# Query, key and value transposes in the tile's own projection banks, in a two-layer trunk kernel

## The chip, the core and the metric

One core of a Trainium2 chip runs the whole program. The metric is the device time of one execution in microseconds (us), given as the median of several executions. The engines are TensorE (PE in the profile; PEld are its weight loads), VectorE (DVE), ScalarE (ACT), GpSimd (POOL) and SyncE (SP), which issues most of the transfers. Matrix results land in PSUM; the kernel takes it in eight pieces of 128 partitions by 512 float32 numbers, called banks here, two of which it uses together as one tile of 1024.

## The reference

One inference step of a trunk of two layers, on 640 tokens (512 "sample" tokens and 128 "prompt" tokens that share the weights), with model width 2048 and heads of 128. Each layer normalises and modulates its input, takes one wide input projection, mixes, gates, and takes one output projection:

```
hp = rms_norm(xp, norm_g[layer]) * (1.0 + sc_p) + sh_p
hs = rms_norm(xs, norm_g[layer]) * (1.0 + sc_s) + sh_s
qa, ka, va, ga, ub, bb, cb, gb = split_cols(h @ w_in, EVEN_SPLIT)
q = rms_norm(q_heads(qa, A_KV, A_GROUP), qn)
k = rms_norm(kv_heads(ka, A_KV), kn)
o = banded_attend(apply_rope(q, cos, sin), apply_rope(k, cos, sin), v, ctx[0], ctx[1], sink_g)
```

The even layer has banded attention (8 query heads on 2 key heads) and a gated short convolution; the odd layer has a differential attention (8 queries and 8 keys, 4 values of double width) and a dense attention (8 queries on 2 keys). Sample tokens also read 256 cached keys and values per head. Queries and keys are divided by the root of the mean of their squares (QK-norm) and, for sample tokens, rotated. Keys and values of the prompt are outputs too.

## The kernel before

**Tiles.** A job is one tile of 128 projection columns for all 640 tokens. The tile lies with its columns on the partitions, in two halves of 320 tokens, `pa` and `pb`, each in a bank of its own. `new_pp` (L283) hands out the banks: tags `pa0`, `pb0`, `pa1`, `pb1`, one buffer each, or, for one index, the two banks of the score tile S. A tile is the sum over 16 blocks of 128 input features; inputs and weights are split into a high and a low part in float32r, so each block is three matmuls per half (L263 to L265, in parts L277 to L279, 96 matmuls to a tile). `split` writes the high part on ScalarE (L227) and the low part on VectorE (L228); it splits weights (`wh`, `wl`) and everything else alike. Another part of the input projection of the odd layer, and of both output projections, forms two tiles together from sums of blocks (L596 to L598). TensorE does little besides these matmuls.

**PSUM.** Four banks are `pa` and `pb`; two are S, which a block's scores fill (L812 to L814), and out of which the exponentials are taken (`p`, L786); two are places with the tag T (`psT`, L64). All else goes through the two T places: transposes of keys and values to rows (`to_rows`, L621, matmul at L625), sums of squares of a query (L708), their transposes (L716), transposes of `p` (L800, split to `pth` and `ptl`), a block's output (L860 to L862), and a few sums for the modulation.

**The generators.** When a tile's matmuls are done, its job runs as a generator that is advanced by one step at each slot between quarters of the next tiles:
- `k_gen` (L639) copies the key from its banks to SBUF (`stg`, in `stage`), starts the load of the cached keys (`ctxk`), transposes the five token blocks to rows (L625; four of the sample into one place, the prompt's into another), takes squares on ScalarE and multiplies by the norm's gain on VectorE (`kg`, L657), scales by the root (L664), rotates (`m`, L674), and some slots later transposes back. In that last part the two blocks of the cache (L682), the four of `m` and the last of `kg` (both L625) each take a T place, one after another, and each is split into the key's operands (`k0h`, `k0l`).
- `q_gen` (L692) writes the query and its squares to SBUF (`qx`, `qsq`), rotates it, sums the squares over the partitions by three matmuls with ones (L708, a T place), copies the sums (`qs`, L711), transposes them (L716, another T place), and splits the query.
- `v_gen` and `v_kept` transpose a value to rows through `v_rows` (L737) and split it. `v_gen` is for values that come straight from their banks, `v_kept` for values that were kept in DRAM.
- `pair_gen` takes the ten blocks of scores of two queries.
- Two of the odd layer's keys come back as kept tiles from DRAM (`places` in `k_gen`), with no bank; the others are staged from their banks as in the even layer.

In the first tiles of the even layer six columns are summed up in SBUF (`sums`, TRANS), while two, the first key and another, stay in banks. A fill (`fill0`: L203, L205) works off the modulation weights of later parts on VectorE, in slots of its own rate; its loads (`adaw`, L200) are on SyncE's queue with the weights' (`raw`).

**Order.** The program is written in the order of slots. A scheduler of the framework then sets each engine's order from program order, dependencies and its own model of when a buffer comes free; a tile that waits for a T place may so be moved behind matmuls of the next projection, and another place changes where it stands.

Of the kernel before, what the change touches and what calls it, by code (L numbers as in the profile page):

```python
# [11 lines left out]
F32 = mybir.dt.float32  # L12
# [8 lines left out]
P = 128  # L21
D = 2048
KT = D // P
NS = 512
NP = 128
NT = NS + NP
HALF = NT // 2
CTX = 256
# [22 lines left out]
def trunk_kernel(ctx: ExitStack, tc: tile.TileContext, I: dict, O: dict):  # L51
    nc = tc.nc
    V, A, PE, G = nc.vector, nc.scalar, nc.tensor, nc.gpsimd
# [6 lines left out]
    pproj = ctx.enter_context(tc.tile_pool(name="pproj", bufs=1, space=PSUM))  # L60
# [3 lines left out]
    def psT():  # L64
        return pT.tile([P, 512], F32, tag="T", name="T")
# [21 lines left out]
    ident = const.tile([P, P], F32, name="ident")  # L87
# [138 lines left out]
    def split(hi, lo, x):  # L226
        A.activation(hi, x, AF.Copy)  # L227
        V.tensor_sub(lo, x, hi)  # L228
# [54 lines left out]
    def new_pp(i):  # L283

        if i == 2:
            t = pS.tile([P, 1024], F32, tag="S", name="Sp")
            return t[:, 0:512], t[:, 512:1024]
        return tuple(pproj.tile([P, 512], F32, tag=f"p{h}{i}", name=f"p{h}") for h in "ab")


    prep, attn, early = [], [], []
# [8 lines left out]
    def release(tag):  # L300
        while any(tag in getattr(g, "tags", ()) for g in attn):
            advance(attn, 1)
# [312 lines left out]
    def stage(ap, pp):  # L615
        s = ap.tile([P, NT], F32, tag="stg", name="stg", bufs=2)
        for i, sl in HV:
            A.copy(s[:, sl], pp[i][:, 0:HALF])
        return s

    def to_rows(src, sample):  # L621

        t = psT()
        for i, b in enumerate(range(4) if sample else (4,)):
            PE.transpose(t[:, i * P:(i + 1) * P], src(b), ident)  # L625
        return t if sample else t[:, 0:P]

    def cols_of(t):
        return lambda b: t[:, b * P:(b + 1) * P]
# [9 lines left out]
    def k_gen(ap, pp, tag, src, gain, new_out, then=None, more=0, places=None):  # L639
        def place(c, b, name):  # L640
            if places is None:
                return ap.tile([P, b, P], F32, tag="rp", name=name, bufs=3)
            return places[:, c:c + b, :]

        raw = ap.tile([P, 2, P], F32, tag="ctxk", name="ctxk", bufs=1)
        nc.sync.dma_start(raw, src.rearrange("(c p) d -> p c d", p=P))
        x = stage(ap, pp) if places is None else pp
        yield
        ss = small.tile([P, 5], F32, tag="ss", name="ss")
        kg = place(0, 5, "kg")  # L650
        junk = ap.tile([P, P], F32, tag="junk", name="junk", bufs=1)
        for sample in (True, False):
            t = to_rows(cols_of(x), sample)
            for i, b in enumerate(range(4) if sample else (4,)):
                A.activation(junk, t[:, i * P:(i + 1) * P], AF.Square, accum_out=ss[:, b:b + 1])
            if sample:
                V.tensor_mul(kg[:, 0:4, :], t.rearrange("p (b f) -> p b f", b=4),  # L657
                             gain[:, None, :].to_broadcast([P, 4, P]))
            else:
                V.tensor_mul(kg[:, 4, :], t, gain)  # L660
        r = small.tile([P, 5], F32, tag="r", name="r")
        V.tensor_scalar(ss, ss, 1.0 / P, EPS, ALU.mult, ALU.add)
        G.tensor_tensor(r, ss, half[:, 0:5], op=ALU.pow)
        V.tensor_mul(kg, kg, r[:, :, None].to_broadcast([P, 5, P]))  # L664
        nc.gpsimd.dma_start(new_out, kg[:, 4, :])
        m1, m2 = place(5, 4, "m1"), place(9, 4, "m2")
        x = kg[:, 0:4, :].rearrange("p b (a h f) -> p (b a) h f", a=2, h=2)
        y = m1.rearrange("p b (a h f) -> p (b a) h f", a=2, h=2)
        z = m2.rearrange("p b (a h f) -> p (b a) h f", a=2, h=2)
        V.tensor_mul(y, x, cosR[:, :, None, :].to_broadcast([P, 8, 2, 32]))  # L670
        V.scalar_tensor_tensor(out=z[:, :, 0, :], in0=x[:, :, 1, :], scalar=-1.0, in1=sinR,
                               op0=ALU.mult, op1=ALU.mult)
        V.tensor_mul(z[:, :, 1, :], x[:, :, 0, :], sinR)
        V.tensor_add(m1, m1, m2)  # L674
        for _ in range(2 + more):
            yield
        release(tag)
        hi, lo = (ap.tile([P, 896], F32R, tag=tag + t, name=tag + t) for t in "hl")
        st[tag] = (hi, lo)
        t = psT()  # L680
        for c in range(2):
            PE.transpose(t[:, c * P:(c + 1) * P], raw[:, c, :], ident)  # L682
        split(hi[:, 0:CTX], lo[:, 0:CTX], t[:, 0:CTX])
        t = to_rows(lambda b: m1[:, b, :], True)
        split(hi[:, CTX:CTX + NS], lo[:, CTX:CTX + NS], t)
        t = to_rows(lambda b: kg[:, b, :], False)
        split(hi[:, CTX + NS:CTX + NT], lo[:, CTX + NS:CTX + NT], t)
        if then:
            prep.append(then())


    def q_gen(ap, pp, tag, gain, then=None, wait=True):  # L692
        x = ap.tile([P, NT], F32, tag="stg", name="qx", bufs=2)
        sq = ap.tile([P, NT], F32, tag="stg", name="qsq", bufs=2)
        for i, sl in HV:
            A.activation(x[:, sl], pp[i][:, 0:HALF], AF.Copy, scale=gain)
            A.activation(sq[:, sl], pp[i][:, 0:HALF], AF.Square)
        sw = ap.tile([P, NS], F32, tag="rp", name="qsw", bufs=3)
        for d in range(4):
            A.copy(sw[32 * d:32 * d + 32, :], x[32 * (d ^ 1):32 * (d ^ 1) + 32, 0:NS])  # L700
        V.tensor_mul(sw, sw, sinT)
        m = ap.tile([P, NS], F32, tag="rp", name="qm", bufs=3)
        V.tensor_mul(m, x[:, 0:NS], cosT)
        V.tensor_add(m, m, sw)
        yield
        ss = psT()
        for g, o in enumerate((0, 256, 384)):
            PE.matmul(ss[32 * g:32 * g + 32, 0:256], ones, sq[:, o:o + 256], start=True, stop=True,  # L708
                      tile_position=(0, 32 * g))
        sb = ap.tile([96, 256], F32, tag="qs", name="qs", bufs=1)  # L710
        A.copy(sb, ss[0:96, 0:256])  # L711
        if wait:
            yield
        t = psT()
        for j in range(2):
            PE.transpose(t[:, j * 96:(j + 1) * 96], sb[:, j * P:(j + 1) * P], ident[0:96, 0:96])  # L716

        u = small.tile([P, 6], F32, tag="ss", name="u")
        V.tensor_scalar(u.rearrange("p (j g) -> p j g", j=2),
                        t[:, 0:192].rearrange("p (j g x) -> p j g x", j=2, g=3)[:, :, :, 0], P * EPS, None, ALU.add)  # L720
        release(tag)
        r6 = small.tile([P, 6], F32, tag="r" + tag, name="r" + tag, bufs=1)
        G.tensor_tensor(r6, u, half[:, 0:6], op=ALU.pow)
        r = [r6[:, c:c + 1] for c in (0, 3, 1, 4, 5)]
        hi, lo = (ap.tile([P, NT], F32R, tag=tag + t, name=tag + t) for t in "hl")
        split(hi[:, 0:NS], lo[:, 0:NS], m)
        split(hi[:, SPLIT], lo[:, SPLIT], x[:, SPLIT])
        st[tag] = (hi, lo, r)
        if then:
            attn.append(then())  # L730

    def ctx_load(ap, src, w):
        raw = ap.tile([P, 2, w], F32, tag="ctxv", name="ctxv", bufs=1)
        nc.sync.dma_start(raw, src.rearrange("(c p) d -> p c d", p=P))
        return raw

    def v_rows(ap, x, hi, lo, cols, new_out):  # L737
        t = to_rows(cols_of(x), True)
        split(hi[:, 2:6, cols], lo[:, 2:6, cols], t.rearrange("p (b f) -> p b f", b=4))
        t = to_rows(cols_of(x), False)  # L740
        vp = ap.tile([P, P], F32, tag="vp", name="vp", bufs=1)
        V.tensor_copy(vp, t)
        split(hi[:, 6, cols], lo[:, 6, cols], vp)
        nc.gpsimd.dma_start(new_out, vp)

    def v_tiles(ap, w):
        release("v")
        st["v"] = tuple(ap.tile([P, 7, w], F32R, tag=t, name=t) for t in ("vh", "vl"))
        return st["v"]

    def v_gen(ap, pp, src, new_out):
        x = stage(ap, pp)
        yield
        hi, lo = v_tiles(ap, P)
        split(hi[:, 0:2, :], lo[:, 0:2, :], ctx_load(ap, src, P))
        v_rows(ap, x, hi, lo, slice(0, P), new_out)

    def v_load(i):
        t = pools["cur"].tile([P, NT], F32, tag="vraw", name="vraw", bufs=1)
# [268 lines left out]
    def k_job(tag, src, gain, new_out, *a):  # L1028
        return lambda pp: k_gen(pools["cur"], pp, tag, src, gains[gain], new_out, *a)
# [96 lines left out]
    for i in range(4):  # L1126
        kv, h = i // 2, 2 * i
# [554 lines left out]
    for n in range(1, 4):  # L1682
        h = heads[n]
# [118 lines left out]
```

## Time and profile before

| | |
|---|---|
| median of 3 runs | 2285.19 us (2284.16 to 2288.55) |
| profiled execution | 2283.79 us, its span 2282.0 us |
| TensorE busy | 2249.8 us, 15941 instructions |
| VectorE busy | 1603.5 us, 2830 instructions |
| ScalarE busy | 1087.7 us, 2281 instructions |
| HBM | 150 GB/s over the span |

The span is the part of the profiled execution between its first and its last instruction on the core; the execution's own time is 1.8 us longer. Times in rows are us from the start of the span. A row of the timeline gives a start, the busy time, the engine, the line, the operation with what it writes and reads, how many were joined into the row, and in brackets how long the engine waited ahead of it and for which instruction of which engine. A row of the waits gives the waiting instruction, an arrow, the instruction that ended the wait, and total, count and longest.

### The profile page before, as it was taken

Reading aid. Unit: us, or ns where it says so; the run is one execution under the profiler, and the core shown is the slowest. Engines: PE = TensorE matmul, PEld = TensorE weight load, DVE = VectorE, ACT = ScalarE, POOL = GpSimd, SP = SyncE. Lnnn points to the kernel's source line nnn. Section 1 sums busy time; section 2 is a strip of 40 time slices with the busy share of each in tenths; the row PEclk is TensorE's granted clock in tenths of the full one; section 3 lists DMA queues with packets and bytes.
Section 4 is the critical chain, followed back from the end, with each engine's and each line's share of the span. In section 5 each row is a group of like instructions: output and inputs, shape, how many; then the busy total and the mean of one; then the engine's idle time right before and its main releaser. Section 6 shows DMA issues by size and latency. Waiting matters only on the chain.

```text
span 2282.0 us, 41084 instructions
## 1 busy us (share of the span) xinstructions
PE 2249.8 (99%) x15941; PEld 2172.7 (95%) x15941; DVE 1603.5 (70%) x2830; ACT 1087.7 (48%) x2281; POOL 162.1 (7%) x226
## 2 busy tenths in 40 slices
PE   7999999999999999999999999999999999999999
PEld 5889999999999999999999999999999999999999
DVE  5666969779779777887797666566666655557765
ACT  5224545244352222544474444465565676755443
POOL 1001000000000000000100001111111100000101
PEclk9999999999999999999999999999999999999999
DMA  9975555555537564855553334423223211238642
GB/s 322 318 227 181 171 155 170 184 155 172 179 112 242 176 190 142 273 171 148 165 166 102 116 116 115 141 65 100 85 62 99 71 55 58 74 102 272 183 136 62
DMA packets 385395, 344.20 MB, mean 151 GB/s; under 512 B 16418, under 2 KB 342528, under 8 KB 384688
## 3 DMA queue, kind: packets, MB, share of 16 engines
q1 hardware_dynamic: 370624, 296.66, 43.5%
q0 software_dynamic: 13856, 42.76, 5.4%
q8 instruction: 125, 2.05, 0.4%
q10 hardware_dynamic: 720, 2.16, 0.3%
q14 instruction: 70, 0.57, 0.1%
HBM read 301.93 MB, written 39.59 MB: 150 GB/s over the span
## 4 chain that ended last, share of the span: by engine, by line
PE 48%; ACT 3%; DVE 2%; DMA 2%; issue 2%; POOL 0%; SPq 0%; POOLq 0%; DVEq 0%; ACTq 0%
PE pq L598 7%; PE pq L597 7%; PE pq L596 7%; PE pb L278 2%; PE pb L277 2%; PE pb L279 2%; PE pa L277 2%; PE pa L279 2%; PE pa L278 2%; PE T L800 1%; PE S L812 1%; PE T L625 1%; PE S L814 1%; PE S L813 1%; ACT qsw L700 1%
## 5 line engine op out<-in xcount | busy, mean ns | idle before, releaser
L227 ACT ACTIVATE wh<-raw 128x512 fp32r<-128x512 f32 x418 | 263.6, 631 | 550.7 <-PE pb L264 393.6
L228 DVE TENSOR_TENSOR wl<-raw,wh 128x512 fp32r<-128x512 f32 x418 | 287.5, 688 | 201.5 <-ACT wh L227 177.7
L263 PE MATMUL pa<-h,wh 128*128 128x320 f32 x978 | 309.9, 318 | 1.8 <-ACT h L227 1.7
L264 PE MATMUL pa<-h,wh 128*128 128x320 f32 x978 | 304.0, 312 | 1.4 <-DVE h L228 1.3
L265 PE MATMUL pa<-h,wl 128*128 128x320 f32 x978 | 303.0, 310 | 0.0
L264 PE MATMUL pb<-h,wh 128*128 128x320 f32 x978 | 302.6, 309 | 0.0
L265 PE MATMUL pb<-h,wl 128*128 128x320 f32 x978 | 302.4, 309 | 0.0
L263 PE MATMUL pb<-h,wh 128*128 128x320 f32 x978 | 301.6, 309 | 0.7 <-ACT h L1412 0.7
L205 DVE SCALAR_TENSOR_TENSOR acc<-adaw,sT,acc 128x1024 f32<-128x1024 f32 x240 | 300.1, 1276 | 0.5 <-DMA adaw<-in_ada_w 0.5
L596 PE MATMUL pq<-h,wh 128*128 128x320 f32 x672 | 208.8, 311 | 0.5 <-ACT wh L227 0.5
L598 PE MATMUL pq<-h,wl 128*128 128x320 f32 x672 | 207.9, 309 | 0.2 <-DVE wl L228 0.2
L597 PE MATMUL pq<-h,wh 128*128 128x320 f32 x672 | 207.7, 309 | 0.0
L263 PEld LDWEIGHTS pa<-h,wh 128*128 128x128 f32 x978 | 183.6, 188 | 15.1 <-issue 9.1
L264 PEld LDWEIGHTS pa<-h,wh 128*128 128x128 f32 x978 | 183.8, 188 | 7.2 <-issue 4.1
L263 PEld LDWEIGHTS pb<-h,wh 128*128 128x128 f32 x978 | 183.3, 188 | 1.4 <-ACT h L1412 0.9
L264 PEld LDWEIGHTS pb<-h,wh 128*128 128x128 f32 x978 | 183.6, 188 | 0.9 <-issue 0.8
L265 PEld LDWEIGHTS pa<-h,wl 128*128 128x128 f32 x978 | 183.7, 188 | 0.4 <-issue 0.4
L265 PEld LDWEIGHTS pb<-h,wl 128*128 128x128 f32 x978 | 183.6, 188 | 0.0
L598 PE MATMUL pq<-T,wl 128*128 128x320 f32 x504 | 155.1, 308 | 0.2 <-DVE wl L228 0.2
L596 PE MATMUL pq<-T,wh 128*128 128x320 f32 x504 | 155.2, 308 | 0.1
L597 PE MATMUL pq<-T,wh 128*128 128x320 f32 x504 | 155.2, 308 | 0.0
L277 PE MATMUL pa<-h,wh 128*128 128x320 f32 x448 | 146.1, 326 | 0.0
(463 smaller groups left out, 5408.1 us busy)
## 6 DMA issues: line engine op xcount, KB each, us to landing
adaw<-in_ada_w SPq DMA_DIRECT2D x128, 512.0 KB, 4.2
raw<-in_ev_w_in SPq DMA_DIRECT2D x176, 256.0 KB, 3.3
raw<-in_od_w_in SPq DMA_DIRECT2D x154, 256.0 KB, 2.9
ada<-in_ada_w SPq DMA_DIRECT2D x32, 1024.0 KB, 9.7
w<-in_od_w_in SPq DMA_DIRECT2D x27, 512.0 KB, 3.9
yd<-y POOLq DMA_DIRECT2D x32, 320.0 KB, 3.5
yin<-yd SPq DMA_DIRECT2D x32, 320.0 KB, 4.5
w<-yd SPq DMA_DIRECT2D x32, 320.0 KB, 4.2
```

The source lines that it names most:

```text
L205: V.scalar_tensor_tensor(out=acc[c], in0=w, scalar=sT[:, kt, c:c + 1], in1=acc[c], op0=ALU.mult, op1=ALU.add)
L227: A.activation(hi, x, AF.Copy)
L228: V.tensor_sub(lo, x, hi)
L263: PE.matmul(ps, wh[:, i, :], hi[:, sl], start=(j == js[0] if alone else (pos == 0 and j == 0)), stop=False)
L264: PE.matmul(ps, wh[:, i, :], lo[:, sl], start=False, stop=False)
L265: last_mm[j % 4] = PE.matmul(ps, wl[:, i, :], hi[:, sl], start=False, stop=(j == js[1] - 1 if alone else (pos == 3 and j == 3)))
L277: PE.matmul(ps, wh[:, j, :], hi[:, sl], start=(qd == 0 and j == 0), stop=False)
L278: PE.matmul(ps, wh[:, j, :], lo[:, sl], start=False, stop=False)
L279: PE.matmul(ps, wl[:, j, :], hi[:, sl], start=False, stop=(qd == 3 and j == 3))
L596: PE.matmul(ps, wh[:, j, :], hi, start=(new and h == 0 and j == 0), stop=False, **kw)
L597: PE.matmul(ps, wh[:, j, :], lo, start=False, stop=False, **kw)
L598: PE.matmul(ps, wl[:, j, :], hi, start=False, stop=(h == 1 and j == 3), **kw)
```

## The change

Four edits. A list `whole` holds the projection tiles that have banks of their own (not those in S or in SBUF), and `bank_of(pp, i)` gives bank `i` of such a tile, or a T place for any other. With it
- `k_gen` transposes a key's sample rows into the key's own `pa` and its prompt rows into its own `pb`;
- `q_gen` puts the sums of squares into the query's own `pa` and their transposes into its own `pb`;
- `v_gen` transposes a value's rows into its own `pa` and `pb`;
- in the last part of `k_gen` the last block of `kg` goes into the T place of the two cache blocks (L690, L691), so that two places are used where there were three, and it is split ahead of `m`.

Lines from 286 on stand 8 lower in the kernel after (L708 is L716 there, L625 is L633). The number of instructions of every engine stays the same but for waits.

```diff
@@ -285,7 +285,15 @@
         if i == 2:
             t = pS.tile([P, 1024], F32, tag="S", name="Sp")
             return t[:, 0:512], t[:, 512:1024]
-        return tuple(pproj.tile([P, 512], F32, tag=f"p{h}{i}", name=f"p{h}") for h in "ab")
+        pp = tuple(pproj.tile([P, 512], F32, tag=f"p{h}{i}", name=f"p{h}") for h in "ab")
+        whole.extend(pp)
+        return pp
+
+    whole = []
+
+    def bank_of(pp, i):
+
+        return pp[i] if any(t is pp[i] for t in whole) else psT()
 
 
     prep, attn, early = [], [], []
@@ -618,9 +626,9 @@
             A.copy(s[:, sl], pp[i][:, 0:HALF])
         return s
 
-    def to_rows(src, sample):
-
-        t = psT()
+    def to_rows(src, sample, t=None):
+
+        t = psT() if t is None else t
         for i, b in enumerate(range(4) if sample else (4,)):
             PE.transpose(t[:, i * P:(i + 1) * P], src(b), ident)
         return t if sample else t[:, 0:P]
@@ -650,7 +658,7 @@
         kg = place(0, 5, "kg")
         junk = ap.tile([P, P], F32, tag="junk", name="junk", bufs=1)
         for sample in (True, False):
-            t = to_rows(cols_of(x), sample)
+            t = to_rows(cols_of(x), sample, bank_of(pp, 0 if sample else 1))
             for i, b in enumerate(range(4) if sample else (4,)):
                 A.activation(junk, t[:, i * P:(i + 1) * P], AF.Square, accum_out=ss[:, b:b + 1])
             if sample:
@@ -680,11 +688,11 @@
         t = psT()
         for c in range(2):
             PE.transpose(t[:, c * P:(c + 1) * P], raw[:, c, :], ident)
+        PE.transpose(t[:, CTX:CTX + P], kg[:, 4, :], ident)
         split(hi[:, 0:CTX], lo[:, 0:CTX], t[:, 0:CTX])
+        split(hi[:, CTX + NS:CTX + NT], lo[:, CTX + NS:CTX + NT], t[:, CTX:CTX + P])
         t = to_rows(lambda b: m1[:, b, :], True)
         split(hi[:, CTX:CTX + NS], lo[:, CTX:CTX + NS], t)
-        t = to_rows(lambda b: kg[:, b, :], False)
-        split(hi[:, CTX + NS:CTX + NT], lo[:, CTX + NS:CTX + NT], t)
         if then:
             prep.append(then())
 
@@ -703,7 +711,7 @@
         V.tensor_mul(m, x[:, 0:NS], cosT)
         V.tensor_add(m, m, sw)
         yield
-        ss = psT()
+        ss = bank_of(pp, 0)
         for g, o in enumerate((0, 256, 384)):
             PE.matmul(ss[32 * g:32 * g + 32, 0:256], ones, sq[:, o:o + 256], start=True, stop=True,
                       tile_position=(0, 32 * g))
@@ -711,7 +719,7 @@
         A.copy(sb, ss[0:96, 0:256])
         if wait:
             yield
-        t = psT()
+        t = bank_of(pp, 1)
         for j in range(2):
             PE.transpose(t[:, j * 96:(j + 1) * 96], sb[:, j * P:(j + 1) * P], ident[0:96, 0:96])
 
@@ -734,10 +742,10 @@
         nc.sync.dma_start(raw, src.rearrange("(c p) d -> p c d", p=P))
         return raw
 
-    def v_rows(ap, x, hi, lo, cols, new_out):
-        t = to_rows(cols_of(x), True)
+    def v_rows(ap, x, hi, lo, cols, new_out, banks=(None, None)):
+        t = to_rows(cols_of(x), True, banks[0])
         split(hi[:, 2:6, cols], lo[:, 2:6, cols], t.rearrange("p (b f) -> p b f", b=4))
-        t = to_rows(cols_of(x), False)
+        t = to_rows(cols_of(x), False, banks[1])
         vp = ap.tile([P, P], F32, tag="vp", name="vp", bufs=1)
         V.tensor_copy(vp, t)
         split(hi[:, 6, cols], lo[:, 6, cols], vp)
@@ -753,7 +761,7 @@
         yield
         hi, lo = v_tiles(ap, P)
         split(hi[:, 0:2, :], lo[:, 0:2, :], ctx_load(ap, src, P))
-        v_rows(ap, x, hi, lo, slice(0, P), new_out)
+        v_rows(ap, x, hi, lo, slice(0, P), new_out, [bank_of(pp, i) for i in range(2)])
 
     def v_load(i):
         t = pools["cur"].tile([P, NT], F32, tag="vraw", name="vraw", bufs=1)
```

The scheduler sets another order with it. Below is what stands in a row on an engine at three places; `[waits ...]` names what the instruction waits for, and "x3" joins equal ones.

TensorE at the first key of the even layer, before. `stg` is the staged key, `ctxk` its cached keys, `kg` the key in rows; `pb<-h_...` is the end of one projection tile, and `pa<-h_469` the first block of the next in the key's banks.

```order
L625 MATMUL T<-ident,stg 128x128 [waits PE_49]
...
L263 MATMUL pb<-h_2059,wh 128x320
L264 MATMUL pb<-h_2059,wh 128x320
L265 MATMUL pb<-h_2059,wl 128x320
L263 MATMUL pa<-h_469,wh 128x320
L264 MATMUL pa<-h_469,wh 128x320
L265 MATMUL pa<-h_469,wl 128x320 [waits DVE_49]
```

The same place after.

```order
L633 MATMUL pa<-ident,stg 128x128 [waits Activation_49]
L633 MATMUL pa<-ident,stg 128x128
L633 MATMUL pb<-ident,stg 128x128
...
L265 MATMUL pb<-h_2059,wl 128x320
L690 MATMUL T<-ident,ctxk 128x128 [waits DMAHW5_49,PE_49]
L690 MATMUL T<-ident,ctxk 128x128
L263 MATMUL pa<-h_469,wh 128x320 [waits DVE_49]
...
L263 MATMUL pa<-h_764,wh 128x320
L691 MATMUL T<-ident,kg 128x128 [waits DVE_49]
```

The key's transposes lie in `pa` and `pb` and wait for no matmul of before; the opening matmul of the next tile now waits for VectorE, the cache's transposes stand 16 projection matmuls earlier, ahead of it, and the transpose of `kg` stands ten matmuls behind the opener, 39 matmuls earlier than before.

TensorE in the odd layer at a query, before. `qsq` are the query's squares; `pth`, `pb<-h_13104` and the like belong to the attention block and to the projection that run beside it (numbers of buffers differ between the two kernels: 13104 there is 13084 here).

```order
L279 MATMUL pa<-h_13120,wl 128x320
L277 MATMUL pa<-h_13128,wh 128x320
L278 MATMUL pa<-h_13128,wh 128x320
L279 MATMUL pa<-h_13128,wl 128x320
L708 MATMUL T<-qsq,ones 32x256 [waits DVE_49]
L708 MATMUL T<-qsq,ones 32x256 x2
L277 MATMUL pb<-h_13104,wh 128x320
L278 MATMUL pb<-h_13104,wh 128x320
L279 MATMUL pb<-h_13104,wl 128x320
L860 MATMUL T<-pth,vh 128x256 [waits Activation_49]
```

The same place after.

```order
L808 MATMUL T<-ident,p 128x128 x3
L277 MATMUL pb<-h_12827,wh 128x320
L278 MATMUL pb<-h_12827,wh 128x320
L279 MATMUL pb<-h_12827,wl 128x320
L716 MATMUL pa<-qsq,ones 32x256 x3
L277 MATMUL pa<-h_13084,wh 128x320
...
L277 MATMUL pb<-h_13084,wh 128x320
L278 MATMUL pb<-h_13084,wh 128x320
L279 MATMUL pb<-h_13084,wl 128x320
L868 MATMUL T<-pth,vh 128x256 [waits Activation_49]
```

The sums stand ahead of the twelve `pa` matmuls instead of behind them, and wait for nothing new; the next block's L860 (L868) stands where it stood.

VectorE in the even layer from the first instruction of the fill, before. `nm` is a score's maximum, `l` and `rl` its sum and reciprocal, `acc` the fill's accumulators.

```order
L203 TENSOR_SCALAR acc_2931<-adaw,sT 128x1024 [waits DMAHW0_49,DMASW3_49,DMASW2_49]
L790 TENSOR_TENSOR l<-l,es 128x1 [waits Activation_49]
L203 TENSOR_SCALAR acc_2932<-adaw,sT 128x1024
L792 RECIPROCAL rl<-l 128x1 [waits DVE_49]
L205 SCALAR_TENSOR_TENSOR acc_2931<-adaw,sT,acc_2931 128x1024 [waits DMAHW1_49]
L779 TENSOR_REDUCE nm<-S 128x1 [waits PE_49]
L228 TENSOR_TENSOR wl<-raw,wh 128x512 [waits DMAHW5_49,Activation_49]
L783 TENSOR_SCALAR nm<-nm,rq_2705,nsink 128x1 [waits DVE_49,Pool_49]
```

The same place after.

```order
L203 TENSOR_SCALAR acc_2928<-adaw,sT 128x1024 [waits DMAHW0_49,DMASW3_49,DMASW2_49]
L203 TENSOR_SCALAR acc_2929<-adaw,sT 128x1024
L798 TENSOR_TENSOR l<-l,es 128x1 [waits Activation_49]
L205 SCALAR_TENSOR_TENSOR acc_2928<-adaw,sT,acc_2928 128x1024 [waits DMAHW1_49,DVE_49]
L800 RECIPROCAL rl<-l 128x1 [waits DVE_49]
L205 SCALAR_TENSOR_TENSOR acc_2929<-adaw,sT,acc_2929 128x1024
L787 TENSOR_REDUCE nm<-S 128x1 [waits PE_49]
L228 TENSOR_TENSOR wl<-raw,wh 128x512 [waits DMAHW5_49,Activation_49]
L791 TENSOR_SCALAR nm<-nm,rq_2702,nsink 128x1 [waits DVE_49,Pool_49]
```

Each step of the fill stands one place earlier, so that ahead of the second `nm` stand two L205 where there was one.

## The prediction

> **What bounds the kernel now.** I read the page first, then TensorE's waits by line, then the timelines around each wait.
>
> ```profile
> PE 2249.8 (99%) x15941; PEld 2172.7 (95%) x15941; DVE 1603.5 (70%) x2830; ACT 1087.7 (48%) x2281; POOL 162.1 (7%) x226
> PEclk9999999999999999999999999999999999999999
> 1200.00:1300.00 100.00, 100.00 (x684) 100.00 (x683) 68.03 (x103) 46.07 (x88) 4.32 (x8) 1.00 0.36 111
> ```
>
> The last row is one stretch: its length, then busy us and instructions of TensorE, its weight loads, VectorE, ScalarE and GpSimd, the clock, DMA share and GB/s. TensorE is busy nearly all of the 2282.0 us at a full clock. In an undisturbed stretch 684 matmuls start in 100 us: 0.146 us a step, which prices an early or late place in its order. The change adds no work (engine by engine the order has as many instructions as before), so it can only move TensorE's waits. They are these:
>
> ```profile
> PE T L708 <- DVE ptl L228: 1.5, 3, 0.6
> PE S L812 <- ACT p L786: 1.1, 4, 0.5
> PE T L625 <- DVE k0l L228: 1.0, 1, 1.0
> PE T L708 <- DVE kpl L657: 0.8, 2, 0.4
> PE T L800 <- ACT p L871: 0.7, 1, 0.7
> PE T L625 <- DVE m L674: 0.6, 1, 0.6
> ```
>
> Columns: total us, times, longest. L708 writes a query's sums, L625 a transpose; where they wait for `ptl`, `k0l` or `kpl`, they need none of these, but the T place (one of two) that the named instruction still reads. That is 1.5 + 0.8 + 1.0 = 3.3 us. The `m` wait is for data.
>
> **The change: q sums.** For 22 of the 24 queries the sums go to bank pa of the query's own projection (the other two have theirs in SBUF, so no bank). In the order shown above for the query near 1896 us the wait on VectorE is gone, and the sums stand 11 or 12 matmuls earlier at three such places (L708 is L716 now).
>
> ```profile
> 1895.66 0.69 DVE L228 TENSOR_TENSOR ptl<-T,pth 128x512 fp32r<-128x512 f32 x1
> 1896.41 0.63 PE L708 MATMUL T<-qsq,ones 128*32 128x256 f32 x6 [0.52 <-DVE ptl L228]
> 1897.39 0.35 ACT L711 COPY qs<-T 96x256 f32<-96x256 f32 x1
> 1897.52 0.28 PE L860 MATMUL T<-pth,vh 128*128 128x256 f32 x1
> ```
>
> `ptl` ends at 1896.35 and frees the place. What is late next is L860 to L862, which read this `pth` and `ptl`; 0.52 us earlier they would start at 1897.00, still behind `ptl`. So the wait goes and does not come back: 2.3 us in the five places (1.5 + 0.8).
>
> **Key's third place.** The last key transpose (`kg`) joins the cache's two in one place.
>
> ```profile
> 462.82 0.60 PE L625 MATMUL T<-ident,m 128*128 128x128 f32 x4
> 464.73 0.31 PE L264 MATMUL pa<-h,wh 128*128 128x320 f32 x1
> 465.58 1.01 DVE L228 TENSOR_TENSOR k0l<-T,k0h 128x256 fp32r<-128x256 f32 x2
> 466.05 0.33 PE L625 MATMUL T<-ident,kg 128*128 128x128 f32 x1 [1.01 <-DVE k0l L228]
> 466.51 0.31 PE L264 MATMUL pb<-h,wh 128*128 128x320 f32 x1
> 1555.94 0.31 PE L277 MATMUL pa<-h,wh 128*128 128x320 f32 x1
> 1556.21 0.33 PE L625 MATMUL T<-ident,kg 128*128 128x128 f32 x1
> 1556.66 0.31 PE L277 MATMUL pa<-h,wh 128*128 128x320 f32 x1
> 1566.93 0.66 PE L625 MATMUL T<-ident,m 128*128 128x128 f32 x4
> ```
>
> In a row of four a transpose takes (0.60 - 0.27)/3 = 0.11 us, 0.27 being one alone as recorded. Alone between projection matmuls, `kg` cost 464.73 to 466.51 less three steps of 0.146, so 1.34 us, and 0.28 us at 1556. In the row it costs 0.11. That gives 1.34 - 0.11 = 1.2 us once, and 0.17 us at the six other single places, 1.0 us. At three more places it now stands inside TensorE's wait for `m` (as before 1566.93), so that its 0.11 us goes, 0.3 us in all.
>
> **Remainder.** The second transpose of a query's sums goes to pb and value transposes to pa and pb. The rows of the waits name nothing of size there; I take 0.5 us, with bounds of 0 and 1.0 (the latter twice the wait at 1896). Gains: 2.3 + 1.2 + 1.0 + 0.3 + 0.5 = 5.3 us, with bounds of 4.8 and 5.8.
>
> **What it costs: the first key.** Here the change adds a wait. The order at it is shown above. The opening matmul takes the bank in which the key now lies, only 8 projection matmuls after its transposes, so it waits until VectorE has read the key; and `kg` stands ten matmuls on, waiting for its scaling. Behind these two waits stands the whole projection.
>
> ```profile
> 200.38 0.31 PE L263 MATMUL pa<-h,wh 128*128 128x320 f32 x1
> 201.73 0.69 DVE L657 TENSOR_TENSOR kg<-T,gain_rows 128x512 f32<-128x512 f32 x1
> 204.10 0.82 DVE L664 TENSOR_TENSOR kg<-kg,r 128x640 f32<-128x640 f32 x1 [1.13 <-POOL r L663]
> 208.58 0.66 PE L625 MATMUL T<-ident,m 128*128 128x128 f32 x4 [0.64 <-DVE m L674]
> ```
>
> The opener came at 200.38; with two transposes ahead (0.22) it comes at 200.60 and waits until 202.42: 1.8 us. Ten steps later, at 203.9, it waits for the scaling's end at 204.92: 1.0 us. The old wait for `m` (0.64) goes, since VectorE reaches `m` two weight splits sooner; `kg` and one value transpose standing alone add 0.17. So TensorE is 1.8 + 1.0 - 0.6 + 0.2 = 2.4 us late here. A part is then absorbed, because two later waits hang on VectorE:
>
> ```profile
> 224.68 0.89 DVE L635 SCALAR_TENSOR_TENSOR y<-gt_t,sum 128x320 f32<-128x320 f32 x2
> 225.63 0.82 SPq L200 DMA_DIRECT2D adaw<-in_ada_w  x2
> 229.90 0.75 DVE L203 TENSOR_SCALAR acc<-adaw,sT 128x1024 f32<-128x1024 f32 x1 [2.08 <-DMA adaw<-in_ada_w]
> 231.38 1.26 DVE L205 SCALAR_TENSOR_TENSOR acc<-adaw,sT,acc 128x1024 f32<-128x1024 f32 x1
> 235.03 0.39 PE L812 MATMUL S<-k0h,q0h 128*128 128x256 f32 x1 [0.54 <-ACT p L786]
> 237.49 0.88 PE L800 MATMUL T<-ident,p 128*128 128x128 f32 x6 [0.67 <-ACT p L871]
> 240.00:300.00 60.00, 60.00 (x434) 59.08 (x434) 57.68 (x99) 25.47 (x56) 1.66 (x3) 1.00 0.60 181
> ```
>
> The fill (L203, L205, the modulation weights) starts when its first load lands, 4.27 us after L635 lets it go. L635 follows the second query's sums, but ScalarE's order there is looser now; I take 0.8 us late, between 0 and 2.4. And VectorE's order moved, as shown above: one L205 more (1.26) stands ahead of the second score's maximum. So this chain runs 0.8 + 1.26 = 2.0 us late, about as late as TensorE, and the two waits shrink little. But the six transposes of 237.49 now stand four matmuls (0.6 us) later, so work fills that wait: TensorE leaves it 2.0 - 0.6 = 1.4 us late. Bounds: 0.7 (load not late at all) and 3.0 (load late by the full 2.4). I take 1.4.
>
> **Sum.** -5.3 + 1.4 = -3.9 us. The profiled execution took 2283.79 (2282.0 of span and 1.8 around it), 1.4 below the median of 2285.19; applied to the median, 2281.3 us. 0.2% is 4.6 us, about the spread of the three runs (4.4 us) and what a measurement of this kernel can tell from no change.
>
> **The rule of the Trainium skill that speaks against this.** At all other tiles the order leaves 60 to 72 matmuls, 8.8 to 10.5 us, between the last sums or transposes in a bank and the projection that takes it next, and at 1897.39 the reader came one us after the sums. The Trainium skill (Perfetto Trace Analysis, Optimizing Tensor Performance) says that independent groups of matmuls should rotate through different PSUM banks, so that emptying one overlaps the next. By that rule the projections would wait. The trace bears it out for the first key alone.
>
> **Rivals.**
> - *The early wait is absorbed whole.* If VectorE's slack after 230 us takes it up, as it would if the load were not late and the fill fell behind, -5.3 us: 2279.9. For it: two waits lie there. Against it: VectorE is busy 57.68 of 60 us behind. Chance 0.15.
> - *The sums' waits come back.* If the transposes of the next block wait in their stead, 2.3 us is not gained: -1.6 us, 2283.6. For it: ScalarE and VectorE feed the same blocks. Against it: L860's inputs above. Chance 0.22.
> - *Slower: VectorE's queue becomes the bound from 230 to 300 us.* If each of the eight scores after the first two waits behind one more L205, 8 x 1.26 = 10.1 us on top of -3.9: 2291.4. It decides where TensorE's slack per score is under 1.26 us. For it: 57.68 of 60. Against it: the one-off shift of the fill, and no wait of size named there. Chance 0.10.
> - *Slower: the rotation rule everywhere.* 33 tiles have such work in their banks (22 queries, 10 keys, a value). If each of the 32 beside the first key's cost 1.8 us as there, that is 58 us, 2339. For it, only that key's place; against it, 8.8 us of distance and a reader that comes after one. Chance 0.01.
>
> **How the numbers follow.** The forecast has the remaining 0.52, with 2279.5 to 2283.0 as its own range. Faster by over 0.2% means under 2280.6: the first rival and somewhat under half of the forecast, 0.38. Slower: the last two, 0.11. Same: 0.51. The range runs from 2277.5, below the first rival by the runs' spread of about 2 us, to 2287.5, halfway between the second rival and the third; the slower rivals stay out.
>
> **What would show it.** Right: no wait of L716 (L708 before) or `kg` on a T place; near 200 us one of L263 on `kg` of 1.8 us and one of L691 of 1.0; the waits of L820 and L808 near 238 us not longer. Wrong: new waits of L808 or L820 between 238 and 300 us, or of an opening matmul elsewhere on ACT or DVE.

## The result and the profile after

The changed kernel takes 2282.97 us (median of 22 runs, 2280.11 to 2289.43), the kernel before 2285.61 us (22 runs beside them, 2282.78 to 2291.51). The ratio is 0.9986, with a 95% interval from 0.998 to 0.9992: taken of 2285.61 us, that is 3.2 us faster, between 1.8 and 4.6 (the two medians stand 2.64 apart). The forecast was -3.9. In the prediction's own terms, which count 0.2% as a change, this is no change, to which it gave 0.51. The profiled execution took 2283.16 us, only 0.63 less than that of before; why two profiles differ by less than this is a part of what follows.

The page's first line and TensorE's waits after (total us, times, longest), cut to those new or moved by 0.2 us or more in the parts that the text speaks of:

```profile
PE 2250.0 (99%) x15941; PEld 2175.0 (95%) x15941; DVE 1602.0 (70%) x2830; ACT 1087.4 (48%) x2281; POOL 162.5 (7%) x226
```

```profile
PE pa L263 <- ACT h L227: 2.5, 5, 1.0
PE pa L264 <- DVE h L228: 2.1, 6, 0.5
PE pa L263 <- DVE kg L665: 1.7, 1, 1.7
PE pq L604 <- ACT wh L227: 1.4, 1, 1.4
PE S L820 <- ACT p L794: 1.3, 4, 0.7
PE T L1594 <- DVE on L1588: 1.0, 1, 1.0
PE T L633 <- DVE qm L711: 1.0, 1, 1.0
PE T L691 <- DVE kg L672: 0.8, 1, 0.8
```

TensorE is as busy as before. The rows in which L708 waited for `ptl` and `kpl`, the one of `k0l` (together 3.3 us) and that of `m` (0.6) are gone. In their place stand the two forecast at the first key, 1.7 and 0.8, and one that was not forecast: 1.0 at L633, put down to `qm`. The rows of `h` and `wh` grew too (before: 1.7, 1.3 and 0.5). They are waits for split inputs and weights and not for the reader of a bank, so they are not the sign of a wrong forecast that the prediction names; they lie in two stretches, 922 to 1453 and 2067 to 2140 us, in which the kernel before differs as much from itself (below). That of `on`, a result of the odd layer's attention, was 0.7 before. The timeline at the first key:

```profile
200.56 0.38 PE L690 MATMUL T<-ident,ctxk 128*128 128x128 f32 x2
202.66 0.41 PE L263 MATMUL pa<-h,wh 128*128 128x320 f32 x1 [1.71 <-DVE kg L665]
204.07 0.31 PE L263 MATMUL pa<-h,wh 128*128 128x320 f32 x1
205.16 0.33 PE L691 MATMUL T<-ident,kg 128*128 128x128 f32 x1 [0.78 <-DVE kg L672]
207.67 0.61 PE L633 MATMUL T<-ident,m 128*128 128x128 f32 x4
```

The opening matmul waits for the reader of its bank, and `kg` for its scaling; `m` no longer waits. At the place near 466 us, and at the query near 1896 us:

```profile
464.27 0.38 PE L690 MATMUL T<-ident,ctxk 128*128 128x128 f32 x2
464.49 0.27 PE L691 MATMUL T<-ident,kg 128*128 128x128 f32 x1
464.59 0.60 PE L633 MATMUL T<-ident,m 128*128 128x128 f32 x4
```

```profile
1893.23 0.63 PE L716 MATMUL pa<-qsq,ones 128*32 128x256 f32 x6
1896.09 0.28 PE L868 MATMUL T<-pth,vh 128*128 128x256 f32 x1
```

`kg` stands in a row with the others, 0.10 us before `m`, where it had waited 1.01. The sums stand twelve matmuls earlier with no wait, and L868, which was next, has none either.

**A finer measure than the median.** The projection matmuls stand in the same order in every kernel here, 12552 of them, so the start of the n-th can be compared between two profiles. I call "lag" its start in one profile less its start in the first profile of before. The lag is level over hundreds of us and steps where something differs; most steps repeat from profile to profile within 0.05 us. The table gives the step of the lag over five stretches (us of before's profile), and within the fourth that at 1486 to 1493:

| profile | 198-274 | 274-922 | 922-1453 | 1453-2067 | of it 1486-1493 | 2067-2140 |
|---|---|---|---|---|---|---|
| changed kernel | +1.47 | -1.18 | +1.74 | -4.58 | +0.75 | +1.76 |
| after_again | +1.84 | -1.13 | +1.73 | -4.88 | +1.11 | +0.75 |
| before_again | -0.28 | +0.06 | +2.46 | +0.18 | -0.01 | +2.87 |
| q_only | -0.22 | +0.05 | +0.73 | -2.57 | +0.43 | -0.10 |
| q_again | -0.22 | +0.03 | +1.20 | -2.70 | +0.28 | -0.77 |
| merge_only | -0.28 | -1.13 | +1.45 | -1.27 | 0.00 | +0.83 |
| k_only | +1.71 | 0.00 | +1.08 | -0.78 | +0.30 | +2.43 |
| k_again | +1.25 | +0.10 | +0.56 | -1.05 | -0.06 | +2.13 |
| v_only | 0.00 | +0.08 | +2.26 | +0.14 | +0.02 | +0.62 |
| first_old | +0.13 | -1.19 | +2.01 | -4.16 | +1.23 | -1.68 |
| first_T | -0.13 | -1.21 | +0.81 | -4.81 | +0.67 | -1.40 |
| first_T_again | -0.13 | -1.16 | +1.17 | -4.03 | +0.89 | +2.99 |

The kernel before, profiled again, steps by +2.46 and +2.87 in the third and the last stretch, where the change does nothing. These two are chance of one execution, and they are about as large as the change: this is why two profiles are no measure of it. The other stretches together give 1.47 - 1.18 - 4.58 = -4.3 us for the changed kernel and -4.2 for its second profile, in line with the ratio.

### The profile page after: what moved, and what is told of

It is laid out like the page before. It is cut to its first block, busy times and chain, and to the rows that moved or that the text cites. A ratio compares the mean times of both kernels' runs of the same rounds, so it can differ in the third digit from the quotient of the medians.

```text
span 2281.4 us, 41068 instructions
## 1 busy us (share of the span) xinstructions
PE 2250.0 (99%) x15941; PEld 2175.0 (95%) x15941; DVE 1602.0 (70%) x2830; ACT 1087.4 (48%) x2281; POOL 162.5 (7%) x226
## 4 chain that ended last, share of the span: by engine, by line
PE 86%; DMA 4%; issue 4%; DVE 3%; ACT 2%; POOL 0%; SPq 0%; POOLq 0%; DVEq 0%; ACTq 0%
PE pq L606 7%; PE pq L605 7%; PE pq L604 7%; PE pa L263 6%; PE pa L264 6%; PE pb L264 6%; PE pa L265 6%; PE pb L263 6%; PE pb L265 6%; PE pa L277 3%; PE pb L278 2%; PE pb L277 2%; PE pb L279 2%; PE pa L279 2%; PE pa L278 2%
## 5 line engine op out<-in xcount | busy, mean ns | idle before, releaser
L205 DVE SCALAR_TENSOR_TENSOR acc<-adaw,sT,acc 128x1024 f32<-128x1024 f32 x240 | 299.9, 1276 | 0.0
```

The costliest lines, as they stand in the source:

```text
L205: V.scalar_tensor_tensor(out=acc[c], in0=w, scalar=sT[:, kt, c:c + 1], in1=acc[c], op0=ALU.mult, op1=ALU.add)
```

## The experiments

Theory A is that of the prediction: a wait for a T place goes for good, and the first key pays for its bank. The rivals are named in each expectation. Times were taken in five rounds beside the kernel before, except in q_again and k_again.

**q_only.** The queries' part alone:

```diff
-        ss = psT()
+        ss = bank_of(pp, 0)
...
-        t = psT()
+        t = bank_of(pp, 1)
```

> The kernel before with the change of the queries alone (sums to pa, their transposes to pb); keys and values as before. Lag means the start of a projection matmul less the start of the same matmul in the profile of before. Theory A (a wait for a T place is gone for good): the lag falls by 0.4 to 0.6 us at each of the five places (1456, 1473, 1848, 1897, 1974 us), 2.5 us together, and nowhere else; ratio to before 0.9989. Theory B (the waits come back at the transposes behind them): the lag recovers within 10 us of each place, sum under 0.5 us, ratio 1.0000.

Measured: the lag falls by 0.49, 0.47, 0.43, 0.58 and 0.62 us at the five places, 2.6 together, and stays level after each. Ratio 0.998 (0.9971 to 0.9988), somewhat more than the steps of -2.6 and -2.7 us give (0.9988). Theory B falls. Smaller steps, 0.17 at 1524 us the largest, add 0.4; against them stands +0.43 near 1487 us, which neither theory had.

**merge_only.** The keys' last three transposes in two places, nothing else:

```diff
+        PE.transpose(t[:, CTX:CTX + P], kg[:, 4, :], ident)
         split(hi[:, 0:CTX], lo[:, 0:CTX], t[:, 0:CTX])
+        split(hi[:, CTX + NS:CTX + NT], lo[:, CTX + NS:CTX + NT], t[:, CTX:CTX + P])
...
-        t = to_rows(lambda b: kg[:, b, :], False)
```

> The kernel before with the last part of the keys alone changed (the prompt block in the place of the cache's two). Theory A (one place less to wait for): -1.2 us at 466 and 0.1 to 0.3 us at each of the other key places of the odd layer, 1.9 together; near the first key the order puts the prompt block 25 matmuls earlier, so that TensorE waits for the scaling there: +0.5 to +1.0. Net -2.3 us, ratio 0.9990. Theory B (the shared place is held longer, until the scaling is there, and the transposes behind it wait instead): the gains are given back at each key, net 0, ratio 1.0000.

Measured: -1.22 us at 466, -1.27 in the odd layer, ratio 0.9991 (0.9982 to 1.0). Theory B falls. Two of A's numbers were off. In the odd layer I had taken 1.9 from steps of the changed kernel to which, as k_only shows, the keys' rows add. And near the first key nothing is lost: TensorE in this kernel waits there for `kg`, start to start 0.86 us more than usual, but no longer for `m`, which had cost 0.80 so; the lag even falls by 0.3, as it does in before_again.

**first_old.** The whole change, with the first key as before (`own` is true for the first key alone):

```diff
-            t = to_rows(cols_of(x), sample, bank_of(pp, 0 if sample else 1))
+            t = to_rows(cols_of(x), sample, psT() if own else bank_of(pp, 0 if sample else 1))
...
+        if own:
+            t = to_rows(lambda b: kg[:, b, :], False)
+            split(hi[:, CTX + NS:CTX + NT], lo[:, CTX + NS:CTX + NT], t)
```

> The whole change, save that the first key alone keeps its rows and its last three transposes in T places as before. Theory A (the first key costs 1.5 us for good): the lag at 274 us is 0 and not +1.5; the rest as in the changed kernel, so 1.5 us under it: ratio to before 0.9980. Theory C (the time lost at the first key is slack that later waits on VectorE would have taken anyway): the lag at 274 us is like the changed kernel's within 0.3 us, same time as it, ratio 0.9986.

Measured: +0.13 us over 198 to 274, against +1.47 and +1.84 with the first key changed; median 2279.97 us against 2281.48 for the changed kernel beside it (after_again); ratio 0.9972 (0.996 to 0.9983). Theory C falls. TensorE at this place, where the old wait is back and the opening matmul (200.47) has none:

```profile
200.47 0.31 PE L263 MATMUL pa<-h,wh 128*128 128x320 f32 x1
208.77 0.66 PE L633 MATMUL T<-ident,m 128*128 128x128 f32 x4 [0.73 <-DVE m L684]
209.27 0.27 PE L633 MATMUL T<-ident,kg 128*128 128x128 f32 x1
```

**after_again** and **before_again.** Both kernels unchanged, profiled a second time.

> The changed kernel unchanged, profiled once more. Theory A (the steps of the lag at 925 to 963, 1486 to 1493 and 2066 to 2131 us, +1.8, +0.75 and +1.8, are chance of one execution): these differ by 0.5 us or more from the first profile's, while the first key (+2.1, then -0.6), 466 (-1.2) and the five sums (-2.5) repeat within 0.1 us each. Theory D (they are effects of the change): all steps repeat within 0.2 us. Ratio 0.9986 in both.

> The kernel before unchanged, profiled once more. Theory A (the steps of the lag at 925 to 963, 1486 to 1493 and 2066 to 2131 us belong to chance, and the first profile of before happened to be quick at 925 to 963): the lag here steps by +1 to +2 us at 925 to 963 and by some tenths to 1.5 us elsewhere in these three places, and by less than 0.1 us at all others. Theory D (they belong to the change): no step over 0.3 us anywhere. Ratio 1.0000.

Measured: after_again repeats the first key up to 221 us (+2.09 twice), 466 and the five sums within 0.04 us; ratio 0.9977 (0.9967 to 0.9987). By itself it could not tell chance from effect, since 922 to 1453 came out alike. before_again does: theory D falls for 922 to 1453 and 2067 to 2140 (+2.46, +2.87 with no change at all). TensorE's wait in the latter stretch, first in before's first profile, then in the second:

```profile
PE pq L596 <- ACT wh L227: 0.5, 1, 0.5
```

```profile
PE pq L596 <- ACT wh L227: 2.4, 1, 2.4
```

But near 1487 us before_again is -0.01, so there D was right and A wrong: it is an effect of the change.

**k_only.** The keys' rows in their own banks, last part as before:

```diff
-            t = to_rows(cols_of(x), sample)
+            t = to_rows(cols_of(x), sample, bank_of(pp, 0 if sample else 1))
```

> The kernel before with the rows of the keys alone in the keys' own banks; the last three transposes take three places as before. Theory A: the opening matmul at 201 us waits 1.8 us for the gain, the prompt block waits for nothing, so the lag is +1.0 to +1.3 at 221 us and about +0.8 at 274; -0.36 at 1923 to 1930; net +0.5 us, ratio 1.0002. Theory E (keys' own banks save T places at all ten keys, and the first key's cost is the prompt block's alone): lag 0 at 274 us, and -0.2 us or more at each key of the odd layer.

Measured: +2.00 us at 221, more than A's 1.0 to 1.3; ratio 1.0007 (0.9999 to 1.0016). The opening matmul started 1.88 us late here, and `m` still waited:

```profile
200.58 0.38 PE L690 MATMUL T<-ident,ctxk 128*128 128x128 f32 x2
202.59 0.41 PE L263 MATMUL pa<-h,wh 128*128 128x320 f32 x1 [1.63 <-DVE kg L665]
208.62 0.63 PE L633 MATMUL T<-ident,m 128*128 128x128 f32 x4 [0.77 <-DVE m L682]
```

So it was the order of the merged last part, not the earlier cache, that had taken the wait for `m` away. VectorE shows how: its last addition for `m` starts at 206.83 us in the changed kernel and at 206.38 in merge_only, with two weight splits behind it that stood ahead of it before, where it started at 207.85; here it starts at 207.78. The bank alone costs 1.9. In the odd layer E is partly right: -0.27 us at four places (before's first is 1545 us), of which the one near 1802 is lost again at 1808, where TensorE waits for `on` itself (0.7 us before, 1.0 here), and -0.36 at 1923 to 1930. At those four nothing of the key itself had waited, but the transposes of `on`, for the T places that the keys' rows had taken (near 1925 us the order itself moved by 4 to 8 matmuls). In before:

```profile
1544.82 0.31 PE L279 MATMUL pb<-h,wl 128*128 128x320 f32 x1
1545.17 0.44 PE L1586 MATMUL T<-ident,on 128*128 128x128 f32 x2
```

The first transpose starts 0.35 us behind the matmul, where a step is 0.146. VectorE's reading of the key's rows in the T place (L657) ends at 1545.11, just ahead of it; in k_only the transpose follows its matmul by 0.15.

**v_only.** The values' rows in their own banks, nothing else (`v_rows` with the banks of the tile).

> The kernel before with the values' rows alone in the values' own banks; TensorE's order is as before. Theory A: no step of the lag over 0.1 us but at the three places of chance; ratio 1.0000. Theory G (a value's rows hold up the next tile's opening matmul as the first key's do): +1 us or more at a value of the even layer, ratio 1.0005 or over.

Measured: no step of note outside the places of chance; ratio 1.0001 (0.9992 to 1.0009). Theory G falls.

**first_T.** The whole change, with the first key's rows in T places, and its last part in two places:

```diff
-            t = to_rows(cols_of(x), sample, bank_of(pp, 0 if sample else 1))
+            t = to_rows(cols_of(x), sample, psT() if own else bank_of(pp, 0 if sample else 1))
```

> The whole change, save that the first key's rows go to T places; its last three transposes take two places, as in the changed kernel. After the run with that last part alone, theory A expects here what it gave near the first key (lag -0.3 at 274 us) and the rest of the changed kernel: about 0.3 us under the run in which the whole first key is as before, 1.8 under the changed kernel, ratio 0.9972. Theory F (the 1.5 us at the first key belong to the early order of the prompt block and not to the banks): the lag at 274 us is over +0.5.

> The whole change with the first key's rows in T places, once more. Theory A: each step of the lag as in the first profile within 0.1 us outside the three places of chance, the value load near 1487 us at 3.8 to 4.3 us by theory H and at 3.1 by theory I; ratio to before 0.997, under the changed kernel's.

Measured: -0.13 us over 198 to 274 in both profiles, so theory F falls. Medians 2278.55 and 2279.85 us; ratios 0.9969 (0.9957 to 0.9981) and 0.9974 (0.9958 to 0.999). By its steps this is the fastest version, 1.6 to 2.0 us under the changed kernel and 0.3 under first_old; by the times alone that is not shown, since the intervals of the three kernels overlap.

**q_again** and **k_again**, for the value load near 1487 us.

> The queries' change alone, profiled once more, for the value load near 1487 us, which is issued as soon as TensorE has read the value before it and for which TensorE waits. From issue to the transposes it took 3.11 to 3.15 us in four profiles without the queries' or the keys' rows in banks, 3.54 here, 3.42 with the keys alone, 3.78 to 4.34 with both. Theory H (the change makes this load slower, since the loads ahead of it stand nearer): 3.4 to 3.7 again. Theory I (chance): 3.1.

> The rows of the keys alone in their banks, profiled once more. Theory H (the change makes the value load near 1487 us slower): 3.3 to 3.6 us from issue to the transposes again. Theory I (chance): 3.1. The first key again costs 2.0 us up to 221 us (1.9 at the opening matmul, and the wait for the rotated key stays, 0.9).

Measured, from the issue of the load to the transposes that need it: 3.39 us with the queries alone (H), 3.06 with the keys alone (I; its first profile had 3.42), 4.00 in first_T_again (H). At the first key k_again repeats k_only: +1.96 us up to 221 us. The rows in before and in first_old:

```profile
1484.00 0.34 SPq L760 DMA_DIRECT2D vraw<-vd  x1
1484.42 0.40 SPq L734 DMA_DIRECT2D ctxv<-in_cache_c_v  x1
1487.12 0.73 PE L625 MATMUL T<-ident,vraw 128*128 128x128 f32 x5 [0.21 <-DMA vraw<-vd]
```

```profile
1483.81 0.34 SPq L776 DMA_DIRECT2D vraw<-vd  x1
1484.24 0.39 SPq L750 DMA_DIRECT2D ctxv<-in_cache_c_v  x1
1488.15 0.74 PE L633 MATMUL T<-ident,vraw 128*128 128x128 f32 x5 [1.44 <-DMA vraw<-vd]
```

The buffer of `vraw` is single, so its load is issued only when TensorE has read the value before, and TensorE has other work for about 2.7 us. A load of 3.1 us costs it 0.4, one of 4.3 costs 1.6. In the changed kernel the row of L633 put down to `qm` in the waits is this wait. The whole change, with the first key in any of its three forms, makes it slower: 3.78 to 4.34 us in five profiles, against 3.11 to 3.15 in the four without the queries' or the keys' rows in banks. For the queries' part alone (3.39 and 3.54) it is likely but less sure, since the keys alone gave 3.06 and 3.42. Why is not shown. The pair of weight loads ahead of it is issued 5.0 us before it in the five, 5.1 with the queries alone and 5.5 to 5.6 in the other six, so it may share the transfer engines with more of them; that was not tried by itself.

## Why the prediction was right

**The q sums** were priced at 2.3 us and gave 2.6 at the five places; measured by the wait alone the term left out what a wait costs from start to start. The rival that the waits come back is refuted by q_only.

**The key's third place** was priced at 1.2, 1.0 and 0.3. Near 466 us it gave 1.22, the other places together 1.27 (merge_only). This term holds as it was worked out.

**The remainder** was taken at 0.5 us for the queries' second transposes and the values. The values gave nothing (v_only), the queries' smaller steps 0.4, and what was missed is the keys' rows in the odd layer, about 1.0: the rows of before showed it, in waits of 0.20 at `on` that I had not put down to a T place taken by a key.

**The first key** was priced at 2.4 us late, of which 1.4 stay. Late it came out at 2.09: the opening matmul 1.96 from start to start, `kg` 0.94, less 0.80 for `m`. That `m` no longer waits was put down to VectorE's order, and the rows under k_only bear it out. But more of it stayed than forecast, 1.5 to 1.8. The step that was mis-sized is the fill, of which I took the load 0.8 us late. VectorE after, in the rows that answer to those of before:

```profile
226.00 0.88 DVE L643 SCALAR_TENSOR_TENSOR y<-gt_t,sum 128x320 f32<-128x320 f32 x2
231.16 1.41 DVE L203 TENSOR_SCALAR acc<-adaw,sT 128x1024 f32<-128x1024 f32 x2 [1.08 <-DMA adaw<-in_ada_w]
232.56 1.28 DVE L205 SCALAR_TENSOR_TENSOR acc<-adaw,sT,acc 128x1024 f32<-128x1024 f32 x1
233.83 1.26 DVE L205 SCALAR_TENSOR_TENSOR acc<-adaw,sT,acc 128x1024 f32<-128x1024 f32 x1
235.01 0.68 DVE L787 TENSOR_REDUCE nm<-S 128x1 f32<-128x512 f32 x1
```

L643 ends 1.3 us later than in before and L203 starts 1.26 later (1.58 in after_again), so the load is as late as the instruction that lets it go. With the second L205, which the order showed, the second maximum is 2.45 us late, not 2.0. So this chain is later than TensorE, where the prediction had it about as late. TensorE then waits longer for the score (0.69 us, and 1.07 in after_again, against 0.54), which the prediction had said it would not, and no longer for the six transposes (0.67 before), as it had said:

```profile
237.44 0.39 PE L820 MATMUL S<-k0h,q0h 128*128 128x256 f32 x1 [0.69 <-ACT p L794]
239.90 0.87 PE L808 MATMUL T<-ident,p 128*128 128x128 f32 x6
```

The four later matmuls ahead of the six transposes give back 0.58 us in each of the four profiles with the first key's rows in its banks; 0.6 was forecast. The wait for the score varies from profile to profile: it steps by +0.15 and +0.53 us in the two of the changed kernel, +0.47 and +0.06 with the keys alone, and -0.30 in before_again with no change at all. So 1.5 and 1.8 us stay. The rival that all is absorbed falls with first_old. The rival of VectorE's queue falls too: from 250 to 274 us the lag moves by 0.04.

**Not foreseen** was the value load near 1487 us, +0.75 and +1.11 us in the two profiles of the changed kernel.

Together: -3.0 (queries) - 1.2 - 1.3 (third place) - 1.0 (keys' rows) + 1.65 (first key) + 0.9 (value load) = -3.95 us, against -4.3 and -4.2 from the steps of the two profiles and -3.2 (-1.8 to -4.6) from the ratio. The forecast of -3.9 is right in sign, size and mechanism, though its agreement to the tenth has two errors of about one us in it, the keys' rows and the value load, that cancel.

With 8 projection matmuls between the transposes and the next use of the bank the opening matmul lost 1.9 us (k_only); at all other tiles, with 60 to 72 between, the profile has no row of an opening matmul that waits for such a reader. So the rule that was weighed, that independent groups should rotate through banks (the Trainium skill, Perfetto Trace Analysis, Optimizing Tensor Performance), decides at one tile here.

## What to carry to other kernels

A bank whose tile has been copied out is a free place for small results, as long as the order leaves its reader time before the next tile opens it: count the matmuls between, tile by tile, and leave out the one where there are few (here it cost 1.5 to 1.8 us of a gain of some 6). A wait that is put down to an unrelated instruction is often one for a place; what it is worth is its start-to-start excess, and other users of the same places gain too. Where the order of the main work is the same, compare two profiles instruction by instruction: single steps of 0.1 us can be read where whole times scatter by several us.

## What the runs showed of the hardware

Two executions of the same program differ most at a few places: over 2067 to 2140 us the lag of the two profiles of first_T stepped by -1.40 and +2.99 us, and over 922 to 1453 that of before_again by +2.46, while over 274 to 922 the profiles of kernels with the same work agree within 0.1. A load of 320 KB issued in the same place of the program took 3.1 us up to its use in the kernel before and 3.8 to 4.3 with the whole change. A transpose alone between projection matmuls cost 0.28 us and one in a row of transposes 0.11, as taken in the prediction.
